# Product g by seven smaller products in ten chunks, w_out's sums by accumulating DMAs, and an instruction order worked out at build time

## The chip, the cores and the metric

One core of a Trainium2 chip runs the kernel. The metric is the time on the device in microseconds (us): the median of three runs of the kernel before is 777.73 us (777.39 to 778.22). PE is the matrix engine, DVE, ACT and POOL are the vector, scalar and GpSimd engines, and SP is the engine that issues nearly all DMAs.

## The reference

With DEPTH = 1 only the gated short convolution is computed, for 1024 tokens of width 1024, in float32:

```
u = x * rsqrt(mean(x*x) + eps) * pre_norm
z, bg, cg, v = split(u @ w_in, 4)              # w_in: 1024 x 8192, four parts of 2048 columns
y = bg * causal_conv3(cg * v) * silu(z)
m = y @ w_out                                  # w_out: 2048 x 1024
out = x + m * rsqrt(mean(m*m) + eps) * post_norm
```

## The kernel before

**Precision.** A float32 operand is split in a high part (a cast on ACT) and a low part (source minus high part, on DVE). One product of two operands is three matmuls: low by high, high by low, high by high. Where both inputs of the low part's subtraction would lie in SBUF, the kernel can first copy the source to a PSUM bank named `beside` on ACT (`split_by_bank`, lines 183 to 188), so that DVE reads one input from PSUM.

**Tiling of w_in.** The 2048 inner columns are 16 chunks c of 128. A chunk has two pairs p of weight blocks: p = 2c holds (cg, v), p = 2c+1 holds (z, bg). A pair is a 2 x 2 matrix (two column types by two halves of the 1024 rows), and so is u (two halves of the rows by two halves of the tokens). The 2 x 2 product is worked out with seven block products a to g instead of eight (`product`, line 215), on sums and differences of blocks. The sums of w (named se, sc, sf and the difference that overwrites a raw block) are made on POOL (`add_s`, lines 143 to 159). Each of the seven is 4 steps of k by 3 matmuls, 12 matmuls of 128 x 512, into a PSUM bank. What comes out is copied to SBUF by ACT (`snap`, 232) or added by DVE (`after`, from 241).

**One level deeper.** Products b (from chunk 2) and f (chunks 3 to 14) are themselves 2 x 2, over both pairs of a chunk, and are worked out by seven smaller products of 6 matmuls of 128 x 256 (`deep_product`, 779; sums of w on POOL in `deep_sums`, 746; splits in `deep_prep`, 761; results in `deep_after`, 802, and `deep_after_f`, 818). `by_seven` (172) says where. The deeper operands of u stand in tiles with the tag `ub`.

**After a chunk.** The gate cg times v is written in `gpad` (line 281), three convolution taps go over 1024 columns (one on ACT, 674, two on DVE, 683), and products with bg and silu(z) give y's chunk, which goes to DRAM (`y_done`, 290). w_out's product has the same form (seven block products, two of them one level deeper), so sums of y's chunks are made on DVE (`add_y`, 302) and stored.

**w_out's sums.** They do not depend on x. In pairs 8 to 23 `fetch_t` (320) loads rows of w_out, and `add_t` (332) makes the sums: for the large products d, e, g and c by 32 subtractions of 128 x 512 on DVE (355), each stored to DRAM (`t_d`), for the deeper ones by 256-wide subtractions on POOL (342 to 350). They are read again at the end (`load_unit`, 847).

**Order.** The scheduler is switched off: each engine's instructions stand in the order in which the Python code calls them. The order of PE's products is the list `slots` (line 958), and `prepare` (1003) calls the splits of w 7 us ahead of their slot. Buffers of 128 x 512 words come from one pool of PAGES = 36 pages; an instruction or a load that needs a page waits until one is free. After the last pair comes w_out's product (`out_mm`, 1130, and `small_mm`, 1213), with its loads, splits and the second norm in `BESIDE` (1297). SP issues all loads and stores from one queue, in order.

Of the kernel before, what the change touches and what calls it, by code (L numbers as in the profile page):

```python
# [1 line left out]

# [6 lines left out]
F32 = mybir.dt.float32  # L9
# [6 lines left out]
PAGES = 36  # L16
DEEP = 2
DEEP_F = 3
LEAD = 7.0
BY_BANK_DEEP = (("b", 0), ("b", 1), ("b", 2), ("f", 0), ("f", 2))  # L20


@with_exitstack
def kernel(
# [16 lines left out]
    nc = tc.nc  # L41
# [19 lines left out]
    const = ctx.enter_context(tc.tile_pool(name="const", bufs=1))  # L61
    small = ctx.enter_context(tc.tile_pool(name="small", bufs=2))
    up = ctx.enter_context(tc.tile_pool(name="up", bufs=7))
    pages = ctx.enter_context(tc.tile_pool(name="pages", bufs=PAGES))
    psum = ctx.enter_context(tc.tile_pool(name="psum", bufs=8, space=bass.MemoryType.PSUM))
    dram = ctx.enter_context(tc.tile_pool(name="dram", bufs=1, space=bass.MemoryType.DRAM))
# [27 lines left out]
    tx_d = dram.tile([P, 2, CQ, HB // 2], F32, tag="tx_d", name="tx_d")  # L94

# [75 lines left out]

    def by_seven(z, c):

        return c >= DEEP if z == "b" else DEEP_F <= c < NC - 1

# [65 lines left out]
    def after(p, i):  # L241
# [9 lines left out]
        elif i == "d":  # L251
            t = sn[p, "e"]
            nc.vector.tensor_add(t, x_, t)
            if p % 2 and DEEP <= c < DEEP_F:
                for j in range(1, TAPS):
                    conv_tap(c, j)
            elif p == len(PAIRS) - 1 or p % 2 and by_seven("f", c):
                conv_tap(c, TAPS - 1)
            if p % 2:
                nc.gpsimd.tensor_mul(t, t, cvs[c][:, HB:])  # L260
# [10 lines left out]
        elif i == "g":  # L271
            if p % 2:
                cv = cvs[c][:, :HB]
                nc.vector.tensor_mul(cv, x_, cv)
                nc.vector.tensor_mul(cv, cv, sn[p, "a"])
                y_done(c, cvs.pop(c))
            elif c < DEEP:
                start_conv(c)

# [22 lines left out]
    def add_y(c):  # L302
# [6 lines left out]
        else:  # L309
            cv, (t0, t1) = done.pop(c), far_y.pop(c)  # L310
            t2 = page(f"s4_{c}")
            nc.vector.tensor_add(t1, t1, cv[:, HB:])
            nc.vector.tensor_sub(t0, t1, t0)
            nc.vector.tensor_sub(t2, cv[:, :HB], t0)
# [5 lines left out]
    def fetch_t(j):  # L320

        if j >= CH:
            z, k = divmod(j - CH, CQ)
            ts[j] = [page(f"tb{n}_{j}") for n in (0, 1)]
            for n in (0, 1):
                nc.sync.dma_start(ts[j][n], wov[:, CH + k + n * CQ, z * HB : (z + 1) * HB])
            return
        ts[j] = [page(f"t{n}_{j}") for n in range(4)]
        for n, t in enumerate(ts[j]):
            nc.sync.dma_start(t, wov[:, j + n // 2 * CH, n % 2 * HB : (n % 2 + 1) * HB])  # L330

    def add_t(j, steps=range(4)):

        if j >= CH:
            z, k = divmod(j - CH, CQ)
            if 0 in steps:
                ts[j].append(page(f"t23_{j}"))
            b0, b1, t = ts[j]
            l, r = slice(0, HB // 2), slice(HB // 2, HB)
            for n in steps:  # L340
                if n == 0:
                    nc.gpsimd.tensor_sub(b0[:, r], b0[:, r], b0[:, l])
                    nc.sync.dma_start(tb_d[:, z, 0, k], b0)
                elif n == 1:
                    nc.gpsimd.tensor_sub(t[:, l], b1[:, r], b0[:, r])
                elif n == 2:
                    nc.gpsimd.tensor_sub(t[:, r], t[:, l], b0[:, l])
                    nc.sync.dma_start(tb_d[:, z, 1, k], t)
                else:
                    nc.gpsimd.tensor_sub(b1[:, l], b1[:, l], t[:, l])  # L350
                    nc.sync.dma_start(tx_d[:, z, k], b1[:, l])
            return
        t = ts[j]
# [999 lines left out]
```

## Time and profile before

| what | value |
|---|---|
| median of three runs | 777.73 us |
| span of the profiled execution, first to last instruction | 776.2 us |
| median less span | 1.5 us |
| busy: PE, DVE, ACT, POOL | 766.0, 618.4, 436.3, 413.2 us |
| matmuls recorded | 4086 |
| moved by DMA | 127.17 MB, mean 164 GB/s |
| granted PE clock over the span | 0.997 |

No time of the profiled execution itself is given apart from its span; the span and the 1.5 us around it stand for it. A row of the timeline reads: start in us from the span's first instruction, length in us, engine, line, operation, output <- inputs, number of merged instructions, and in brackets the idle time before it with what ended it. A row of the groups has, after the bar, busy us and mean ns of one. A row of the windows gives, for one stretch, its length and the busy us of PE, PE's weight loads, DVE, ACT and POOL, the granted clock, the DMA engines' share and GB/s.

### The profile page before, as it was taken

What the parts mean: (1) busy time and instruction counts of PE and PEld (TensorE: products, weight loads), DVE (VectorE), ACT (ScalarE), POOL (GpSimd) and SP (SyncE); (2) the same over time, 40 slices, a digit from 0 to 9 for tenths busy, and PEclk for the clock granted to TensorE, in tenths of its full rate; (3) what the DMA queues carried; (4) which work ended last, traced back from release to release, by engine and by line L of the source; (5) the groups of instructions that cost most, each with busy time, mean ns of one, the idle gap of its engine ahead of it and who ended that gap; (6) DMA issues with size and microseconds to landing.
All of it is one profiled execution on the core that took longest, in us unless ns stands there. A gap on an engine that the chain in (4) does not pass through costs nothing.

```text
span 776.2 us, 12058 instructions
## 1 busy us (share of the span) xinstructions
PE 766.0 (99%) x4086; PEld 661.8 (85%) x4086; DVE 618.4 (80%) x934; ACT 436.3 (56%) x810; POOL 413.2 (53%) x369
## 2 busy tenths in 40 slices
PE   8999999999999999999999999999999999999996
PEld 6888888888888888888888888888888889889985
DVE  5899786778687878788888887676778899966975
ACT  6764354766556565546465556555544576753821
POOL 2506786937575757575767667373737100850041
PEclk9999999999999999999999999999999999999998
DMA  9210531335463637364847456232325989966345
GB/s 310 71 55 1 149 96 55 96 109 181 138 204 117 210 111 230 111 208 131 257 136 250 138 174 178 96 109 96 115 89 166 336 275 378 309 196 210 112 169 184
DMA packets 115965, 127.17 MB, mean 164 GB/s; under 512 B 7432, under 2 KB 74304, under 8 KB 115904
## 3 DMA queue, kind: packets, MB, share of 16 engines
q1 hardware_dynamic: 115888, 126.41, 50.5%
q8 instruction: 32, 0.52, 0.3%
q14 instruction: 29, 0.24, 0.1%
q10 hardware_dynamic: 16, 0.00, 0.0%
HBM read 91.78 MB, written 34.60 MB: 163 GB/s over the span
## 4 chain that ended last, share of the span: by engine, by line
PE 98%; DVE 1%; DMA 1%; ACT 0%; POOL 0%; issue 0%; POOLq 0%; DVEq 0%; ACTq 0%
PE px L226 15%; PE px L227 15%; PE px L228 15%; PE pv L226 4%; PE pv L227 4%; PE pv L228 4%; PE po_x L1139 4%; PE po_x L1140 4%; PE po_x L1138 4%; PE px2b L800 2%; PE px2b L798 2%; PE px2b L799 2%; PE px2f L800 1%; PE px2f L799 1%; PE px2f L798 1%; PE pp L456 1%
## 5 line engine op out<-in xcount | busy, mean ns | idle before, releaser
L260 POOL TENSOR_TENSOR sne<-sne,cv 128x512 f32<-128x512 f32 x15 | 20.5, 1369 | 122.3 <-DVE cv L683 106.4
L187 ACT COPY beside<-raw 128x512 f32<-128x512 f32 x84 | 49.6, 590 | 29.2 <-DVE dwb1l L188 21.7
L154 POOL TENSOR_TENSOR se<-raw,raw 128x512 f32<-128x512 f32 x31 | 46.8, 1510 | 19.2 <-PE px L228 6.8
L234 ACT COPY sna<-px 128x512 f32<-128x512 f32 x30 | 17.6, 588 | 68.8 <-PE px L228 68.1
L226 PE MATMUL px<-u_d,wdl 128*128 128x512 f32 x124 | 48.7, 393 | 0.0
L226 PE MATMUL px<-u_a,wal 128*128 128x512 f32 x124 | 48.6, 392 | 0.0
L227 PE MATMUL px<-u_a,wah 128*128 128x512 f32 x124 | 48.6, 392 | 0.0
L227 PE MATMUL px<-u_d,wdh 128*128 128x512 f32 x124 | 48.5, 391 | 0.0
L226 PE MATMUL px<-u_g,wgl 128*128 128x512 f32 x124 | 48.4, 391 | 0.0
L227 PE MATMUL px<-u_g,wgh 128*128 128x512 f32 x124 | 48.4, 391 | 0.0
L227 PE MATMUL pv<-u_e,weh 128*128 128x512 f32 x124 | 48.4, 390 | 0.0
L228 PE MATMUL px<-u_d,wdh 128*128 128x512 f32 x124 | 48.4, 390 | 0.0
L226 PE MATMUL pv<-u_e,wel 128*128 128x512 f32 x124 | 48.4, 390 | 0.0
L228 PE MATMUL px<-u_a,wah 128*128 128x512 f32 x124 | 48.3, 389 | 0.0
L227 PE MATMUL px<-u_c,wch 128*128 128x512 f32 x124 | 48.2, 389 | 0.0
L228 PE MATMUL px<-u_c,wch 128*128 128x512 f32 x124 | 48.2, 389 | 0.0
L228 PE MATMUL pv<-u_e,weh 128*128 128x512 f32 x124 | 48.2, 389 | 0.0
L226 PE MATMUL px<-u_c,wcl 128*128 128x512 f32 x124 | 48.2, 389 | 0.0
L228 PE MATMUL px<-u_g,wgh 128*128 128x512 f32 x124 | 48.2, 389 | 0.0
L156 POOL TENSOR_TENSOR sc<-se,raw 128x512 f32<-128x512 f32 x31 | 44.9, 1448 | 5.8 <-issue 3.4
L158 POOL TENSOR_TENSOR sf<-raw,sc 128x512 f32<-128x512 f32 x31 | 46.3, 1493 | 0.0
L355 DVE TENSOR_TENSOR t<-t,t 128x512 f32<-128x512 f32 x32 | 45.8, 1450 | 0.3
(539 smaller groups left out, 2743.7 us busy)
## 6 DMA issues: line engine op xcount, KB each, us to landing
raw<-in_sc_w_in SPq DMA_DIRECT2D x128, 256.0 KB, 4.0
y_d<-cv SPq DMA_DIRECT2D x16, 512.0 KB, 3.2
s_d<-s SPq DMA_DIRECT2D x32, 256.0 KB, 2.9
t<-in_sc_w_out SPq DMA_DIRECT2D x32, 256.0 KB, 2.9
t_d<-t SPq DMA_DIRECT2D x32, 256.0 KB, 3.9
tb<-in_sc_w_out SPq DMA_DIRECT2D x16, 256.0 KB, 4.3
s<-y_d SPq DMA_DIRECT2D x16, 256.0 KB, 4.1
xr<-in_x SPq DMA_DIRECT2D x16, 256.0 KB, 3.8
```

What stands on the lines that cost most here:

```text
L154: nc.gpsimd.tensor_add(t, block(p, 1, 0), block(p, 1, 1))
L156: nc.gpsimd.tensor_sub(t, sums[p, "e"], block(p, 0, 0))
L158: nc.gpsimd.tensor_sub(t, block(p, 0, 1), sums[p, "c"])
L187: nc.scalar.copy(b, src)
L226: nc.tensor.matmul(ps, lo, UH[i][:, k], start=first and k == 0, stop=False, skip_group_check=True)
L227: nc.tensor.matmul(ps, hi, UL[i][:, k], start=False, stop=False, skip_group_check=True)
L228: nc.tensor.matmul(ps, hi, UH[i][:, k], start=False, stop=last, skip_group_check=True)
L355: nc.vector.tensor_sub(t[n], t[a], t[b])
L798: nc.tensor.matmul(ps, lo, uh, start=first and k == 0, stop=False, skip_group_check=True)
L1138: nc.tensor.matmul(ps, lo, u[:, 0, k], start=first, stop=False, skip_group_check=True)
L1139: nc.tensor.matmul(ps, hi, u[:, 1, k], start=False, stop=False, skip_group_check=True)
L1140: nc.tensor.matmul(ps, hi, u[:, 0, k], start=False, stop=last, skip_group_check=True)
```

## The change

**Product g deeper.** g is worked out by seven smaller products too, in chunks 4 to 13. Three of the seven (b', f', g') accumulate straight into the bank of the pair's x product, the other four are copied out and added back to that bank:

```diff
+LAST = {"b": NC, "f": NC - 1, "g": NC - 2}
 def by_seven(z, c):
-    return c >= DEEP if z == "b" else DEEP_F <= c < NC - 1
+    return {"b": DEEP, "f": DEEP_F, "g": DEEP_G}[z] <= c < LAST[z]
...
+elif z == "g" and i in ("b'", "f'", "g'"):
+    ps, first = banks[2 * c + (i == "g'"), "x"][:, HH if i == "f'" else 0 :], False
...
+def deep_after_g(c, i):
+    if i == "g'" and late_conv(c):
+        conv_tap(c, 1)
+    if i in ("b'", "f'", "g'"):
+        return
+    ps = banks[c, "g" + DEEP_C[i][0]][:, :HH]
+    if i == "d'":
+        t, x_ = page(f"gs1_{c}"), banks[2 * c + 1, "x"]
+        nc.scalar.copy(t[:, :HH], ps)
+        nc.vector.tensor_add(t[:, HH:], banks[c, "gv'"][:, :HH], t[:, :HH])
+        nc.vector.tensor_add(x_, x_, t)
+        ...
```

The sums of w for it are four more 256-wide subtractions or additions per chunk on POOL, its splits are plain ones (both inputs in SBUF). Its operands of u are six more `ub` buffers (14 to 20), and PAGES falls from 36 to 30. One of them overwrites a quarter of u_g, which is kept in DRAM (`ug_d`, stored once from SBUF) and restored after chunk 13. In chunks 4 to 13 the gate, the taps and the last products of a chunk come in the next chunk's first pair (`late_conv`).

**w_out's sums.** The 32 loads, 32 subtractions on DVE and 32 stores are gone. `sums_plan` spreads over pairs 9 to 25 (8 sums, each a half of one of e, d, c, g) one DRAM-to-DRAM copy on SP of 1 MB and two DMAs of 512 KB issued by POOL that add in DRAM:

```diff
+def out_sums(p):
+    for to, src, more in SUM_AT.get(p, ()):
+        if more:
+            nc.gpsimd.dma_start(to, src, accum_op=ALU.add)
+        else:
+            nc.sync.dma_start(to, src)
```

Sums take the place of differences, so signs turn: `add_y` uses scalar_tensor_tensor with -1.0 for two of its three steps, and one more ACT instruction multiplies half of the post norm's weights by -1.

**Order.** A class `Plan` stands in front of the engines. From the first planned slot (pair 2) to the end of the last pair it records the calls, works out a due time for each, and issues them in the order of a list scheduling with assumed durations, limited by free pages and PSUM banks; PE's order stays as recorded. Its assumptions, cut:

```diff
+LATE = {"end": 14.0, "store": 6.0, "psum": 3.0}
+SLACK = {"tensor": 1.0, "gpsimd": 0.8, "sync": 1.0, "scalar": 0.1, "vector": 0.1}
+AHEAD = {"sync": 24.0, "gpsimd": 18.0, "scalar": 11.0, "vector": 11.0}
+    ISSUE = {"sync": 0.07, "gpsimd": 1.2, "scalar": 0.1}
...
+    elif where == "tensor":
+        op.dur, op.lat = n / 2400 + 0.0135, n / 2400 + 0.2
+    elif where == "vector":
+        op.dur = 0.1 + n / 960 * (1 if psum or two else 0.55)
+        op.share = 0.0 if psum or not two else 0.4
+    elif where == "scalar":
+        op.dur = 0.1 + n / 1200
+    else:
+        op.dur = 0.16 + n / 390 if n > 8 else 0.1
...
+    if e == "gpsimd" and "dma" in op.name[1]:
+        self.sum_at = t + 15.0
```

The head (norm, transposes, first chunks) and w_out's product keep the order of the calls. Counted in the two built programs: 240 matmuls of 128 x 512 go and 420 of 128 x 256 come; DVE has 33 instructions more (32 subtractions for w_out and 20 low parts of g gone, 30 low parts of 128 x 512, 10 of 128 x 256, 20 sums of 128 x 256 and 20 of 128 x 512 come, and a few for u_g); ACT has 48 more; POOL has 52 compute instructions (four per chunk, four for one further set of sums that no product reads, eight for u_g) and 16 DMA issues more; SP has 50 DMA issues fewer.

More of the change, by code (lines that the diff above doesn't have):

```diff
@@ new lines, with __init__, tile @@
+class Pool:
+    def __init__(self, plan, pool, bufs, space):
+        self.plan, self.pool, self.bufs, self.space, self.gate, self.users = plan, pool, bufs, space, None, []
+    def tile(self, shape, dtype, **kw):
+        t = Tile(self, list(shape), dtype, kw)
+        self.plan.room.setdefault(t.key, kw.get("bufs", self.bufs))
+        if not self.plan.recording:
+            t.get()
+            self.plan.taken.setdefault(t.key, []).append(t)
+        return t
+class Op:
+    __slots__ = ("engine", "name", "args", "kw", "n", "needs", "feeds", "dur", "lat", "waits", "late", "tiles", "news", "start", "ideal", "pos", "share", "soft")
@@ L34 @@
 ):
-    nc = tc.nc
+    nc = plan = Plan(tc.nc)
     P = 128
```

574 lines of the change are left out of this document (471 added, 103 removed).

## The prediction

> **What bounds the kernel now.** I read the page first: the busy times, then the chain that ended last.
>
> ```profile
> span 776.2 us, 12058 instructions
> PE 766.0 (99%) x4086; PEld 661.8 (85%) x4086; DVE 618.4 (80%) x934; ACT 436.3 (56%) x810; POOL 413.2 (53%) x369
> PE 98%; DVE 1%; DMA 1%; ACT 0%; POOL 0%; issue 0%; POOLq 0%; DVEq 0%; ACTq 0%
> ```
>
> PE carries 98% of the chain. A busy PE alone does not prove a gapless PE, so the windows come next: a long one that leaves out head and tail, then two in the middle and one at the start of w_out's product.
>
> ```profile
> core 0: us, PE busy (x) PEld busy (x) DVE busy (x) ACT busy (x) POOL busy (x), PEclk, DMA share, GB/s
> 25.60:770.00 744.40, 744.22 (x3969) 643.71 (x3968) 598.83 (x893) 416.38 (x775) 407.79 (x355) 1.00 0.50 160
> 220.00:260.00 40.00, 40.00 (x220) 34.81 (x219) 32.50 (x47) 22.11 (x40) 27.38 (x26) 1.00 0.55 179
> 460.00:500.00 40.00, 40.00 (x224) 34.97 (x223) 28.93 (x45) 22.41 (x41) 25.89 (x25) 1.00 0.46 142
> 620.00:655.00 35.00, 35.00 (x206) 31.14 (x206) 33.14 (x61) 21.49 (x40) 1.29 (x1) 1.00 0.88 310
> ```
>
> In 744.40 us PE lacks 0.18 us, at a granted clock of 1.00. No wait is left to remove there. Two things follow. A gain can only come from fewer or cheaper matmuls, and what any other engine saves is worth nothing by itself. And every wait that the change brings to PE is added in full. The price of a matmul is its distance to the next one, not its recorded length (0.39 us, which overlaps), so I take starts from the timeline:
>
> ```profile
> 582.76 0.39 PE L226 MATMUL px<-u_g,wgl 128*128 128x512 f32 x1
> 585.48 0.39 PE L226 MATMUL px<-u_c,wcl 128*128 128x512 f32 x1
> 590.92 0.28 PE L798 MATMUL px2b<-u_b,dwb0l 128*128 128x256 f32 x1
> 592.36 0.40 PE L226 MATMUL px<-u_d,wdl 128*128 128x512 f32 x1
> 600.54 0.28 PE L798 MATMUL px2b<-ubch_deep,dwb1l 128*128 128x256 f32 x1
> 601.96 0.40 PE L226 MATMUL px<-u_g,wgl 128*128 128x512 f32 x1
> 610.15 0.28 PE L798 MATMUL pv2b<-u_b,dwb2l 128*128 128x256 f32 x1
> 611.57 0.40 PE L226 MATMUL px<-u_d,wdl 128*128 128x512 f32 x1
> ```
>
> Product g, 12 matmuls of 512, lasts from 582.76 to 585.48, 2.72 us. In the smaller form, a' and b' (12 matmuls of 256) take 1.44 us, c' and e' 1.42, f' and d' 1.42.
>
> **The change on PE.** Per chunk g goes twice: 2 x 2.72 = 5.44 us. Seven small products come, with the operands arranged as for b: 1.44 + 1.42 + 1.42 and half of 1.42 for g', 4.99 us. That is 0.45 us less, 4.5 us in ten chunks. Head, w_out's product and the finish after the last matmul keep their matmuls. If PE stays gapless the span is 776.2 - 4.5 = 771.7 us. The median of the runs lies 777.73 - 776.2 = 1.5 us above the span, so 773.2 us. If all seven cost 0.71 the saving is 4.7, if all cost 0.72 it is 4.0.
>
> All else counts only if PE must wait for it, so the question for each engine is whether its work per chunk still fits in a chunk. A chunk's period now is 37.33 us (POOL's se rows below, 215.36 to 252.69); it becomes 36.88.
>
> **POOL** gets most. Its rows, one chunk of them, and DVE's rows beside:
>
> ```profile
> 215.36 1.75 POOL L154 TENSOR_TENSOR se<-raw,raw 128x512 f32<-128x512 f32 x1
> 222.29 1.07 POOL L752 TENSOR_TENSOR dsf<-sf 128x256 f32<-128x256 f32 x1
> 230.68 1.30 POOL L154 TENSOR_TENSOR se<-raw,raw 128x512 f32<-128x512 f32 x1 [1.52 <-DVE dwb2l L188]
> 235.82 0.92 POOL L342 TENSOR_TENSOR tb<-tb 128x256 f32<-128x256 f32 x1
> 238.40 0.74 POOL L350 TENSOR_TENSOR tb<-tb,t 128x256 f32<-128x256 f32 x1
> 246.80 1.31 POOL L260 TENSOR_TENSOR sne<-sne,cv 128x512 f32<-128x512 f32 x1 [7.66 <-DVE cv L683]
> 248.47 1.35 POOL L1086 TENSOR_TENSOR cv<-snc,sne 128x512 f32<-128x512 f32 x1 [0.35 <-ACT snc L1085]
> 249.78 0.74 POOL L752 TENSOR_TENSOR dsb<-raw 128x256 f32<-128x256 f32 x1
> 252.69 1.74 POOL L154 TENSOR_TENSOR se<-raw,raw 128x512 f32<-128x512 f32 x1
> L355 DVE TENSOR_TENSOR t<-t,t 128x512 f32<-128x512 f32 x32 | 45.8, 1450 | 0.3
> 216.48 2.88 DVE L355 TENSOR_TENSOR t<-t,t 128x512 f32<-128x512 f32 x2
> 225.55 0.68 DVE L192 TENSOR_TENSOR wcl<-sc,wch 128x512 fp32r<-128x512 f32 x1
> 243.65 1.28 DVE L683 SCALAR_TENSOR_TENSOR cv<-gpad,cw,cv 128x1024 f32<-128x1024 f32 x1
> 235.71 0.43 DVE L163 TENSOR_TENSOR dwb<-raw,dwb 128x256 fp32r<-128x256 f32 x1
> L805 DVE TENSOR_TENSOR sna<-px2b,sna 128x256 f32<-128x256 f32 x56 | 23.3, 416 | 3.9 <-PE px2b L800 3.8
> L188 DVE TENSOR_TENSOR wgl<-beside,wgh 128x512 fp32r<-128x512 f32 x24 | 16.4, 685 | 3.9 <-ACT beside L187 3.9
> ```
>
> Four 512-wide sums take 5.14 us (230.68 to 235.82), but 6.93 (215.36 to 222.29) where DVE works on w_out's sums, which themselves take 1.45 us instead of the 0.68 of an equal subtraction (wcl). So an instruction of DVE with two inputs in SBUF and one of POOL hold each other up: 1.79 us on POOL for four of 0.68 us, two thirds of their time. Undisturbed, POOL's chunk is 2 x 5.14 for the sums, 8 x 0.73 for the deeper ones (four from 249.78 to 252.69), 3.3 for tb, and three products of at most 1.35: 23.4 us. By the window it was busy 27.38 x 37.33 / 40 = 25.6, so 2.2 us are disturbance. The g sums add 4 x 0.73 = 2.9. The disturbers change little: 4 x 0.68 = 2.7 us of w_out's sums go, three low parts of 0.68 and one of 0.43 come, 2.5 us. That makes 28.5 us of 36.88.
>
> On top come the 16 accumulating DMAs, two per chunk in chunks 5 to 12. The trace has no DMA that POOL issues. The bounds for its hold on POOL's queue: from below an issue on SP, 1.85 us for four, 0.46 each; from above the landing of a load, 6.0 us, if the queue stood until then (rows below). A negative price is out, since an instruction is added. I take 1.75, the slowest 512-wide POOL row: the instruction stands in POOL's queue like those, and between ends far apart theirs is the nearest row. That is 3.5 us, 32.0 of 36.88 us, and PE feels nothing. If the price is p, POOL is full at p = (36.88 - 28.5) / 2 = 4.2 us; beyond that each further us costs 2 us in each of eight chunks, 16 us.
>
> The Trainium skill, "SBUF — State Buffer", section "Who interferes with whom", says that a DVE instruction with two SBUF inputs and a GpSimd instruction that reads SBUF block each other completely; the two thirds of the rows lean that way.
>
> **DVE.** Out of a chunk go 4 x 1.45 and two low parts of 0.69, 7.2 us. In come 3 x 0.68 + 0.43, two sums of 0.42 (as L805) and two of 0.69 that add to the bank, 4.7; if a disturbed low part takes as long as POOL's slowest row, 1.75, it is 7.9. DVE's 32.50 x 37.33 / 40 = 30.3 us become 27.8 to 31.0 of 36.88. In chunks 12 and 13, which had no such sums, 28.93 x 37.33 / 40 = 27.0 becomes 30.3 to 33.5. It fits.
>
> **ACT** was at 22.11 of 40. Two casts and two copies per chunk go, four casts and three 256-wide copies come, about 1 us: free.
>
> **SP and DMA.** 50 issues fewer, and about the same bytes in the middle, at a DMA share of 0.55: free. A 1 MB copy holds the loads of w behind it back by a few us; the plan lets SP issue up to 24 us ahead of a due time (AHEAD), which covers a copy and a landing of 6.0 us (row B_b below).
>
> **Six pages fewer.** In w_out's product DVE frees a page with each low part, four in 2.48 us (row oy_a), 0.62 each, so a load may start 6 x 0.62 = 3.7 us later. The tightest load there:
>
> ```profile
> 591.25 1.85 SPq L858 DMA_DIRECT2D ru_a<-in_sc_w_out  x4
> B_b<-tb_d SPq DMA_DIRECT2D x8, 256.0 KB, 6.0
> 623.37 2.48 DVE L163 TENSOR_TENSOR oy_a<-ry_a,oy_a 128x512 fp32r<-128x512 f32 x4
> 626.94 1.81 SPq L917 DMA_DIRECT2D B_b<-tb_d  x4
> 642.50 2.18 ACT L162 CAST oB_b<-B_b 128x512 fp32r<-128x512 f32 x4 [4.24 <-DMA s_d<-s]
> ```
>
> Issued by 628.8 and landed 6.0 later, at 634.8, it is used at 642.5: 7.7 us cover 3.7. I cost the pages at nothing there; if that cover were gone, 3.7 us. In the middle the pages are a matter of order.
>
> **The order.** Before, POOL stood 7.66 us behind a tap (row 246.80); a recorded order by due times can fill that. Its assumed durations are near the rows: POOL 512-wide 0.16 + 512/390 = 1.47 against 1.30 to 1.75, DVE 0.63 against 0.68, a matmul 0.227 against 2.72/12 = 0.227. Its margins (0.8 to 1 us for what POOL, SP and PE hand over) are wider than these errors. I cost it at 0, between a gain that PE cannot show and one late operand per chunk.
>
> **The rivals.**
>
> *Part of it is given back.* PE waits 0.15 to 0.3 us per chunk for a low part or a free bank, since four results of g' now pass by ACT and DVE and back into the bank that the next products need, and since DVE runs up to 33.5 of 36.88 us. At 0.3 that is 3 us, 776.2. Against it: the other engines have an eighth or more of the period free.
>
> *All of it is given back*: 0.45 us per chunk, or the 3.7 us of the pages, gives 777 to 778. Also here: the copies and waits behind g' make PE wait exactly where b and f did not.
>
> *POOL becomes the bound.* If it is disturbed by every DVE instruction with two SBUF inputs, as in the four rows at 215.36, and not only by few, its chunk is 23.4 + 2.9 + 2/3 x 11.1 = 33.7 us. The 11.1 are DVE's instructions of that kind after the change: e's and c's low parts (4 x 0.68), two taps (2 x 1.28), three others of 0.68, three of 0.43, and 2.5 for g. Then p above 1.6 us decides. At p = 2.5 a chunk lacks 1.8 us, eight chunks 14 us: 773.2 + 14 = 787 us, slower. Whole blocking instead of two thirds adds 3.7 us to each chunk. For it: the disturbance is in the rows, and issuing is unmeasured. Against it: in the old chunk, with 11.3 us of the same kind and POOL 69% busy, only 2.2 us of disturbance came.
>
> The far end of this rival is that the two exclude each other wholly, wherever they meet. POOL and those DVE instructions then share one time: 26.3 + 11.1 = 37.4 us, over the period even without the DMAs. With p = 1.75 a chunk lacks 4.0 us, eight chunks 32 us, 805 us. The old chunk, 23.4 + 11.3 = 34.7 of 37.33, does not refute it. I give it 5 in 100, within the rival's 25. The rule of the Trainium skill cited above is this far end.
>
> **How the numbers follow.** Forecast, PE gapless within 1 us: 50 in 100, 773.2, its own range 772.4 to 774.3. Partly given back, 774.3 to 776.1: 14. All given back, 776.1 to 779.3: 11. POOL as the bound, above 779.3: 25. A measurement of this kernel can tell about 0.2%, 1.6 us, from no change, so below 776.1 is faster: 64; the same: 11; slower: 25. The range begins at 772.4 (below 773.2 by 0.5 of spread between runs and 0.2 for the cheaper small products, rounded out) and ends at 787, the rival's price at p = 2.5, which leaves out about 15.
>
> **What would show it.** Right: 420 matmuls of 256 with 0.118 to 0.120 us between starts, PE without gaps from 26 us on, its last matmul 4.5 us earlier; POOL at some 32 of 37 us in the middle. Wrong: gaps on PE that end with a low part of se, sc or g late behind a POOL sum (POOL the bound), or behind a load (pages), or with an addition to the x bank (given back). A POOL queue that stands several us at each accumulating DMA would upset the sum most.

## The result and the profile after

The changed kernel takes 791.86 us (median of five runs, 791.77 to 792.4) against 777.73 us for the kernel before on the same chip: 1.0183 times as long, 95% interval 1.0171 to 1.0196. It is slower by 14 us where 773.2 us was forecast, and it lies above the forecast range (772.4 to 787.0). The page of the changed kernel begins with these lines. In this kernel every instruction is issued through `Plan.call`, so all of them carry line 182, and the rows are told apart by their tiles.

```profile
span 790.4 us, 12619 instructions
PE 766.5 (97%) x4266; PEld 666.8 (84%) x4266; DVE 654.5 (83%) x967; ACT 450.0 (57%) x858; POOL 493.5 (62%) x437
```

The windows answer to those of before: the same stretch from 25.60 us to 6.2 us ahead of the span's end, two in the middle, and the start of w_out's product.

```profile
core 0: us, PE busy (x) PEld busy (x) DVE busy (x) ACT busy (x) POOL busy (x), PEclk, DMA share, GB/s
25.60:784.20 758.60, 743.72 (x4148) 647.89 (x4146) 634.38 (x925) 429.68 (x823) 487.81 (x423) 1.00 0.53 160
220.00:260.00 40.00, 37.78 (x227) 33.30 (x226) 35.23 (x51) 22.34 (x43) 32.56 (x30) 1.00 0.57 155
460.00:500.00 40.00, 38.13 (x227) 33.51 (x226) 34.21 (x51) 21.64 (x41) 34.35 (x31) 1.00 0.53 136
634.00:669.00 35.00, 35.00 (x206) 31.15 (x205) 33.12 (x60) 20.39 (x39) 1.47 (x1) 1.00 0.88 299
```

The stretch is 758.60 - 744.40 = 14.2 us longer at the same clock, and PE is no longer gapless in the middle: 2.2 and 1.9 us are missing in the two windows of 40 us. In w_out's product nothing is missing. So the gain is not absent; waits have been put on top of it. With the 4.5 us of the prediction's sum there must be 14.2 + 4.5 = 18.7 us of new waits. The view of waits, rows of PE's weight loads outside the head, has them (tile that waited, what it waited for, us in total, times, longest):

```profile
PEld pv2f L182 <- DVE snc L182: 11.1, 7, 1.8
PEld px2f L182 <- DVE dwf1l L182: 4.5, 5, 1.4
PEld px L182 <- DVE wcl L182: 1.9, 1, 1.9
PEld px L182 <- DVE wgl L182: 1.0, 1, 1.0
```

They add up to 18.5 us, and so do the distances between the starts of PE's matmuls, less what they show in the kernel before. (PE's recorded idle time is smaller, 14.9 us of the stretch, since the record of a matmul, 0.39 us, covers a part of the wait behind it.) In the kernel before none of these four rows exists. The largest is one wait seven times over, once in each of the chunks 5 to 11. Here is one of them in the timeline, first POOL and then DVE and PE:

```profile
232.10 1.74 POOL L182 TENSOR_TENSOR raw<-raw,raw 128x512 f32<-128x512 f32 x1
233.78 1.20 POOL L182 DMA_DIRECT2D t_d<-in_sc_w_out  x1
234.54 1.22 POOL L182 TENSOR_TENSOR dsg<-raw 128x256 f32<-128x256 f32 x1
235.24 1.21 POOL L182 TENSOR_TENSOR dsg<-raw,raw 128x256 f32<-128x256 f32 x1
235.94 1.20 POOL L182 TENSOR_TENSOR dsg<-dsg,raw 128x256 f32<-128x256 f32 x1
237.51 1.65 POOL L182 TENSOR_TENSOR se<-raw,raw 128x512 f32<-128x512 f32 x1 [0.37 <-DVE dwf L182]
234.05 3.38 DVE L182 TENSOR_TENSOR dwf<-sf,dwf 128x256 fp32r<-128x256 f32 x1
237.35 0.68 DVE L182 TENSOR_TENSOR dwg0l<-raw,dwg0h 128x512 fp32r<-128x512 f32 x1
237.95 0.41 DVE L182 TENSOR_TENSOR snc<-px2f,snc 128x256 f32<-128x256 f32 x1
238.29 0.67 DVE L182 TENSOR_TENSOR dwf2l<-beside,dwf2h 128x512 fp32r<-128x512 f32 x1
238.88 0.41 DVE L182 TENSOR_TENSOR snc<-pv2f,snc 128x256 f32<-128x256 f32 x1
239.35 0.38 PE L182 MATMUL pv2f<-u_f,dwf2l 128*128 128x256 f32 x1 [1.48 <-DVE snc L182]
```

The reader is to see five things. POOL issues an accumulating DMA at 233.78, and its three sums for product g follow without a gap, 0.70 us from start to start, though each is recorded with 1.2 us. DVE's low part `dwf` (both inputs in SBUF) starts at 234.05 and takes 3.38 us; it ends with the third sum. Behind it in DVE's queue stands, four places on, the addition that reads the bank pv2f. PE has to write that bank next and waits 1.48 us. And POOL itself then waits for `dwf`, which is what ends its series. The row of this tile over the whole kernel gives minimum, median and maximum of its twelve in ns:

```profile
L182 DVE TENSOR_TENSOR dwf<-sf,dwf x12: 412/3354/3380, 159.0 to 582.0; 128x256 fp32r<-128x256 f32 x12
```

Three take 0.41 to 0.43 us, two 0.96, and seven 3.35 to 3.38. The other places are smaller. At px2f a low part (dwf1l) comes late because the POOL sum it splits (dsf) is late. The early one looks like this:

```profile
59.67 0.10 POOL L182 MEMSET gpad<- 128x2 f32 x1 [23.99 <-DMA ug_d<-xa]
63.39 1.31 DVE L182 TENSOR_TENSOR wel<-se,weh 128x512 fp32r<-128x512 f32 x1 [0.40 <-ACT weh L182]
64.62 1.76 DVE L182 TENSOR_TENSOR wcl<-sc,wch 128x512 fp32r<-128x512 f32 x1
66.44 0.50 PE L182 MATMUL px<-u_c,wcl 128*128 128x512 f32 x1 [1.50 <-DVE wcl L182]
```

POOL's memset waits for the landing of the new store of u_g, and the worked-out order has wel ahead of wcl, which PE needs first. At 576 us the low part wgl stands behind three sums of y in DVE's queue.

### The profile page after: what moved, and what is told of

Read it like the earlier page. It is cut to its first block, busy times and chain, and to the rows that moved or that the text cites. A ratio compares the mean times of both kernels' runs of the same rounds, so it can differ in the third digit from the quotient of the medians.

```text
span 790.4 us, 12619 instructions
## 1 busy us (share of the span) xinstructions
PE 766.5 (97%) x4266; PEld 666.8 (84%) x4266; DVE 654.5 (83%) x967; ACT 450.0 (57%) x858; POOL 493.5 (62%) x437
## 5 line engine op out<-in xcount | busy, mean ns | idle before, releaser
L182 PE MATMUL px<-u_d,wdh 128*128 128x512 f32 x248 | 76.8, 391 | 0.0
L182 PE MATMUL px<-u_a,wah 128*128 128x512 f32 x248 | 76.7, 390 | 0.0
L182 PE MATMUL pv<-u_e,weh 128*128 128x512 f32 x248 | 76.6, 390 | 0.0
L182 PE MATMUL px<-u_c,wch 128*128 128x512 f32 x248 | 76.6, 390 | 0.0
L182 PEld LDWEIGHTS px<-u_d,wdh 128*128 128x128 f32 x248 | 46.6, 188 | 9.3 <-DVE u_d L182 0.2
L182 DVE SCALAR_TENSOR_TENSOR cv<-gpad,cw,cv 128x1024 f32<-128x1024 f32 x32 | 46.8, 1463 | 9.1 <-ACT cv L182 9.1
L182 PEld LDWEIGHTS px<-u_c,wch 128*128 128x128 f32 x248 | 46.7, 188 | 9.1
L182 PEld LDWEIGHTS pv<-u_e,weh 128*128 128x128 f32 x248 | 46.6, 188 | 9.1
L182 PEld LDWEIGHTS px<-u_a,wah 128*128 128x128 f32 x248 | 46.7, 188 | 8.9
L182 POOL TENSOR_TENSOR raw<-raw,raw 128x512 f32<-128x512 f32 x31 | 48.3, 1560 | 0.0
```

Of the source, the lines that this page charges most:

```text
L182: getattr(engine, name)(*(self.plain(a) for a in args), **{k: self.plain(a) for k, a in kw.items()})
```

## The experiments

**Theories.** *Held*: the accumulating DMA, followed at once by POOL sums, keeps a DVE instruction with two SBUF inputs out until the series ends, and DVE's order passes it to PE. Rivals: *Series* (the sums that follow each other do it without a DMA), *Load* (POOL has too much to do, the DMA is beside the point), and for the other 8 us *order* against *load*. Most runs keep the changed kernel's worked-out order and alter it only where `flush` issues it, so that nothing else moves; c1_bank, c2_head, c3_gap and the three runs with a d have their order worked out anew.

**Without POOL's DMAs (a1_no_dma).**

```diff
 for op in order:
+    if op.engine == "gpsimd" and "dma" in op.name[1]:
+        continue
```

> Same instructions in the same order as the changed kernel, except that POOL's 16 accumulating DMAs are left out (the sums of w_out's rows are incomplete, half of each addition is missing). Held (a DMA issued by POOL, followed at once by POOL sums, holds up a DVE instruction with two SBUF inputs until the series ends, and PE gets that through the pv2f bank): dwf falls from 3.38 us to at most 1.5 us, the seven stalls at pv2f (10.8 us) go, 779 to 782 us. Series (the sums that follow each other do it without a DMA): dwf stays above 2.5 us, 790 to 792 us. Load (POOL has too much to do, whatever it is): some 0.8 us of POOL per DMA goes, the stalls behind POOL's late sums shrink all over, those at px2f (3.2 us) as much as those at pv2f: below 779 us.

Measured: 779.54 us (778.84 to 780.02), 12.3 us less, in a kernel that leaves out half of each addition of w_out's rows. The groups of this run (us in all and mean ns before and after the comma) have this row for `dwf`:

```profile
L182 DVE TENSOR_TENSOR dwf<-sf,dwf 128x256 fp32r<-128x256 f32 x12 | 9.9, 823 | 0.0
```

and its waits of PE's weight loads between 200 and 600 us these:

```profile
PEld px2f L182 <- DVE dwf1l L182: 2.2, 3, 0.7
PEld px L182 <- DVE wgl L182: 1.0, 1, 1.0
```

`dwf` falls from 26.7 us in all to 9.9, and the row of pv2f is gone. The sums of g still follow each other without a gap on POOL: Series is refuted. The waits at px2f fall only from 4.5 to 2.2 us, so the DMA's own time on POOL is a small part.

**POOL work in the DMA's place (a2_stand_in).**

```diff
+    if op.engine == "gpsimd" and "dma" in op.name[1]:
+        op.name[0].tensor_sub(*self.scratch)
+        op.name[0].tensor_sub(*self.scratch)
+        continue
```

> In place of each of POOL's 16 DMAs stand two POOL subtractions of 128x224 in SBUF, some 0.65 us each, so POOL has at least as much to do at the same places; w_out's sums are incomplete. Held: no DMA, no hold, dwf at most 1.5 us, no stall at pv2f of over 0.5 us, 779 to 783 us. Series: more sums in a row hold DVE longer, dwf 3.4 us or more, 791 to 794 us. Load: POOL as full as before, 790 to 793 us, whatever dwf takes.

Measured: 784.62 us (784.29 to 785.23). No wait at pv2f and no DVE instruction longer than 1.3 us above its usual time: Load doesn't make the seven waits. But it is 5.1 us more than without the stand-ins, a little outside what Held expected: the waits at px2f rise from 2.2 to 7.1 us in the row of the weight loads. POOL's queue is tight ahead of dsf, where 1.3 us more of anything reach PE.

**Copying instead of adding (a3_plain_dma).**

```diff
+    if op.engine == "gpsimd" and "dma" in op.name[1]:
+        op.kw = {}
```

> POOL's 16 DMAs stay in place with the same rows but copy instead of adding (w_out's sums hold one addend only). Held, by the issue on POOL: dwf stays at 3.4 us, 790 to 792 us. If it is the addition (longer landing, DRAM read and written) that counts: dwf at most 1.5 us and 779 to 782 us. Series and Load: 790 to 792 us, which this run does not tell from Held.

Measured: 787.68 us (787.35 to 788.11). `dwf` takes 2.91 us in the seven chunks, the waits at pv2f are 7.6 us. The time lies between the two forecasts: the hold is there, a little shorter, and the DMA is recorded with 0.73 us instead of 1.19. So in this kernel it is not the adding alone that holds.

**The DMA eight places later (a4_dma_later).** In the order, POOL's DMA ahead of the dsg sums is moved behind the next pair's difference, ahead of sf:

```diff
+    j = next(n for n in pool if any(s.startswith("sf_") for s in names(order[n])))
+    order.insert(j - 1, order.pop(k))
```

> Same instructions, nothing left out; the DMA that POOL issues ahead of the dsg sums (eight of the 16) stands instead behind the next pair's difference, ahead of sf, where POOL has some 4.7 us of idle time. Held: dwf at most 1.5 us, the seven stalls at pv2f go, 779 to 783 us. Series: dwf stays above 2.5 us, 790 to 792 us. Load: POOL's work per chunk is the same, only eight DMAs stand later; the sums ahead come 0.8 us sooner, so part of the stalls goes, 785 to 790 us.

Measured: 788.82 us (788.06 to 789.53), far from the 779 to 783 that Held had. The seven waits at pv2f are gone, but now the second DMA of each chunk waits for the first, POOL has no idle time left behind it, and the hold is there again at another place:

```profile
289.28 1.15 POOL L182 DMA_DIRECT2D t_d<-in_sc_w_out  x1 [4.77 <-issue]
295.90 1.11 POOL L182 TENSOR_TENSOR t<-tb,tb 128x256 f32<-128x256 f32 x1
294.03 4.07 DVE L182 SCALAR_TENSOR_TENSOR cv<-gpad,cw,cv 128x1024 f32<-128x1024 f32 x1 [0.40 <-ACT cv L182]
```

Between the first two rows POOL made six sums without a gap, and a tap of the convolution, 1.28 us when alone, waited for the last of them. In four chunks a tap took 4.0 to 4.8 us. So Held has to be put more widely: not the instruction beside the DMA is held, but any in the series that the DMA begins.

**The disputed instruction by itself (b1_measure, b2_sweep, b3_before).** A program of its own: POOL and DVE start on the same ACT instruction, POOL issues nothing, a copying or an accumulating DMA and then makes subtractions, and DVE makes a 128x256 addition.

```diff
+nc.gpsimd.dma_start(dst[:, case], wov[...], accum_op=ALU.add)
+for n in range(count):
+    nc.gpsimd.tensor_sub(outs[n], a[:, :256], a[:, 256:])
+for _ in range(delay):
+    nc.vector.tensor_add(pp, ps[:, :256], b[:, 256:])   # reads PSUM, 0.46 us apart
+nc.vector.tensor_sub(v, b[:, :256], b[:, 256:])
```

> A program of its own that measures the disputed instruction alone and computes nothing of the reference (the output is a copy of x). In each case DVE starts a 128x256 addition of two SBUF tiles while POOL issues no DMA, a copying DMA or an accumulating DMA of 512 KB in DRAM, and then makes 1, 2, 3, 4, 6 or 8 subtractions of 128x256 in a row (some 0.7 us each); a second set gives DVE one PSUM input. Held: without a DMA the addition takes at most about 1.3 us, however many subtractions; with a DMA it takes about 0.7 us per subtraction more, 2.0 at one, 3.4 at three, 6.9 at eight; with a PSUM input 0.41 us always. Series: it grows with the count without a DMA as well. If neither: at most 1.3 us in all cases, and the 3.4 us of the changed kernel have another cause.

It missed the case: with either DMA DVE's addition started ahead of it and was over before the sums (0.41 to 0.42 us; 0.90 to 0.97 without a DMA). The sweep moves it:

> A program of its own, like the first measurement (nothing of the reference is computed, the output is a copy of x), but DVE's addition of two SBUF tiles, 128x256, starts later by 0.34 us per step, so that it falls into POOL's DMA or among the 8 subtractions behind it; in the first measurement it ended before them. Held in the series: an addition that starts among or ahead of the subtractions behind a DMA takes until the last of them, up to 6 us; without a DMA at most 1.1 us (what is left of one subtraction, and 0.41). With 2 and 4 subtractions it ends with those. If a memset between the DMA and the subtractions ends the hold, at most 1.1 us there, else as without it. A PSUM input: 0.41. The rule that the one that issues first has the pair for its own instruction alone: at most 1.1 us in every case.

The timeline of the sweep, POOL's DMA and series for the first held case, then DVE (the name says kind and number of subtractions; pp are the additions that read PSUM and delay the start):

```profile
160.75 1.15 POOL L56 DMA_DIRECT2D dst<-in_sc_w_out  x1 [0.37 <-issue]
161.52 5.85 POOL L60 TENSOR_TENSOR o<-a 128x256 f32<-128x256 f32 x8
51.34 0.95 DVE L64 TENSOR_TENSOR none8late<-b 128x256 f32<-128x256 f32 x1
105.53 0.91 DVE L64 TENSOR_TENSOR plain8late<-b 128x256 f32<-128x256 f32 x1
161.87 5.79 DVE L64 TENSOR_TENSOR accum8late<-b 128x256 f32<-128x256 f32 x1
204.25 3.62 DVE L63 TENSOR_TENSOR pp<-ps,b 128x256 f32<-128x256 f32 x8
207.79 3.97 DVE L64 TENSOR_TENSOR accum8late<-b 128x256 f32<-128x256 f32 x1
230.87 1.77 DVE L64 TENSOR_TENSOR accum2late<-b 128x256 f32<-128x256 f32 x1
253.10 3.12 DVE L64 TENSOR_TENSOR accum4late<-b 128x256 f32<-128x256 f32 x1
```

An addition that starts among the subtractions behind an accumulating DMA ends 0.3 us after the last of them (161.87 + 5.79 = 167.66 against 161.52 + 5.85 = 167.37), however many there are; in the two starts between it takes 5.4 and 4.9 us. Without a DMA it waits for what is left of one subtraction. With a PSUM input it isn't held: the eight additions from 204.25 on run on at 0.46 us each, though POOL's series begins at 205.59, and the one with two SBUF inputs behind them is caught. A memset between DMA and subtractions doesn't help (5.2 us). The Trainium skill, "SBUF — State Buffer", section "Who interferes with whom", calls the pair of ports that DVE and POOL share an exclusive lock and gives it to whichever issues first, for its whole instruction (it says the latter of DVE's two-port modes). The rows without a DMA agree, at most 0.97 us; the rows behind an accumulating DMA don't, since there DVE waits for up to eight instructions of POOL. Why it waits no run shows.

One thing differs from the kernel. In the two sweeps an addition that started during the accumulating DMA, ahead of the first subtraction, was not held (0.44 to 0.93 us). In the kernel `dwf` starts 0.27 us behind the DMA and 0.49 us ahead of the first sum, and is held. So the programs show that such a series holds DVE, but not every condition for it.

Two questions were left, the copying DMA and what ends a hold:

> A program of its own again (the output is a copy of x): as the sweep, but two subtractions stand ahead of the DMA without a pause, as the difference does in the changed kernel, and six behind it; four cases have a POOL copy that waits for ACT behind three subtractions, and five more subtractions behind that. If the issue on POOL is enough, whatever it does, the copying DMA holds the addition to the end of the series here as the accumulating one does (2.9 us in the changed kernel with copying DMAs), which it did not when POOL was idle ahead of it. If only the accumulating DMA holds, the copying one leaves at most 1.1 us. A pause that POOL makes ends a hold: an addition that starts among the first three takes until the pause, 2 us at most, and one that starts behind the pause at most 1.1 us.

```profile
95.73 0.91 DVE L70 TENSOR_TENSOR plain6late<-b 128x256 f32<-128x256 f32 x1
177.81 4.45 DVE L70 TENSOR_TENSOR accum6late<-b 128x256 f32<-128x256 f32 x1
234.90 2.44 DVE L70 TENSOR_TENSOR pause3late<-b 128x256 f32<-128x256 f32 x1
272.15 0.84 DVE L70 TENSOR_TENSOR pause3late<-b 128x256 f32<-128x256 f32 x1
```

A copying DMA holds nothing here (0.46 to 0.95 us in seven starts). A pause of POOL (here 1.3 us or more) ends the hold: 2.44 us up to it, 0.84 behind it. Why the copying DMA held `dwf` for 2.91 us in the kernel stays open.

**The low part by way of PSUM (c1_bank).**

```diff
-BY_BANK_DEEP = (("b", 0), ("b", 1), ("b", 2), ("f", 0), ("f", 2))
+BY_BANK_DEEP = (("b", 0), ("b", 1), ("b", 2), ("f", 0), ("f", 2), ("f", 3))
```

> Nothing left out. The low part of f's g' operand (dwf, 128x256) is read by way of the PSUM bank, so that DVE needs no second SBUF input there; the order is worked out anew with that. Held: dwf takes 0.41 us, the seven stalls at pv2f shrink to under 0.5 us each, the rest stays (3 us at px2f, 2.4 us early, 1.0 us late): 781 to 785 us; should the next DVE instruction with two SBUF inputs (dwg0l, right behind) be caught instead, 789 to 792 us. Load: POOL's work is unchanged, 790 to 792 us.

Measured: 814.26 us (813.3 to 815.85). `dwf` is free, and the next two-input instruction is caught, and for longer: `dwg0l` takes 5.5 us in three chunks and 7.2 in three more. POOL's `se` waits for `dwf` and so ended the old series; nothing in the series waits for `dwg0l`, so in these last three chunks it runs on over eight instructions.

**Earlier sums ahead of the memset (c2_head).**

```diff
+    add_s(2, "ec")
     head.close()
...
-            add_s(2, "ecdf")
+            add_s(2, "df")
```

> Nothing left out. se and sc of pair 2 are made ahead of the memset of gpad, which waits for the store of u_g; the order behind it is worked out anew. Early stall by that wait: the 2.35 us between 40 and 80 us fall below 0.7 us, the rest stays: 789.5 to 790.5 us. If the stall comes from DVE's order alone (wel ahead of wcl): 791 to 792.5 us.

Measured: 791.9 us (791.1 to 792.02). The early wait is split: by the starts of PE's matmuls 1.8 us between 40 and 80 us instead of 2.3, now at 57.3 and 59.6 us, where PE waits for DVE's low parts of u_g while POOL makes these sums. The memset alone is not the cause.

**DMAs only where POOL will pause (c3_gap).** `pick` may issue a DMA only if no other POOL instruction is due and ready within 1.3 us, and the sums begin at pair 3:

```diff
+if e == "gpsimd" and "dma" in op.name[1] and not pause(op):
+    continue
...
-sums_plan(2 * DEEP_F + 4)
+sums_plan(4)
```

> Nothing left out. POOL's 16 DMAs are all there, but the order is worked out with one more rule: POOL issues one only where none of its other instructions is due and ready within the next 1.3 us, and they may begin at pair 3 instead of 9, so that each chunk has one at a place where POOL then waits. Held in the series: no DVE instruction with two SBUF inputs over 1.5 us, no stall at pv2f, 778 to 781 us. Load: POOL has the same work in all, one DMA less per chunk: 784 to 789 us. A hold by any DMA, wherever it stands: 790 to 792 us.

Measured: 790.29 us (787.42 to 791.86), in the range of "a hold by any DMA". But no DVE instruction is held (none over 1.3 us above its usual time), and yet the time is about that of the changed kernel: in the new order POOL runs without a pause from 329 to 353 us, its dsf is late, and the waits at px2f are 7.6 us. It tells nothing against the hold, but it shows that an order without holds can lose as much elsewhere.

**DMAs sooner (d1_soon).**

```diff
-self.sum_at = t + 15.0
+self.sum_at = t + 9.0
...
-SUM_AT.setdefault(p0 + 2 * j + k, []).append(...)
+SUM_AT.setdefault(p0 + j, []).append(...)          # p0 = 3
```

> Nothing left out. POOL's 16 accumulating DMAs and their eight copies come sooner, two per pair in pairs 3 to 10 and at least 9 us apart, so that most of them lie in chunks 1 to 4, where POOL has less to do, and chunks 6 to 14 have none; the order is worked out anew. Held: a hold can still come in chunks 1 to 5, none later; the stalls at pv2f from 270 us on go, what stays is about that of the run without DMAs: 779 to 784 us. If POOL's time in the early chunks is as short as later: 784 to 790 us. Load with no part played by the DMAs: 790 to 792 us.

Measured: 809.52 us (808.67 to 809.69). Nine DVE instructions take 2.1 to 5.3 us, all behind DMAs in chunks 1 to 6; behind 280 us, where there are no DMAs, 3 us of waits are left. Held had forecast a gain of some 10 us, and a loss of 18 came: it failed in sign as well as in size. What fits it is only where the holds are. In the early chunks POOL's series were no shorter, so that more instructions than before were caught, nine instead of seven.

**g undone, and pages (d2_no_g, d3_no_g_36).**

```diff
-DEEP_G = 4
+DEEP_G = 99
...
-PAGES = 30
+PAGES = 36          # second run only, with 14 instead of 20 ub buffers
```

Both runs also leave out g's deeper operands of u and the store and restoring of u_g.

> Product g is worked out by twelve matmuls of 512 again in every chunk (its sums, splits, operands of u and the store of u_g are gone); POOL's DMAs, the worked-out order and 30 pages stay. Without waits it would take the 777.7 us of the kernel before. Held: dwf, dwg and dsg no longer meet behind a DMA as before, but other sums follow the DMAs; where a DVE instruction with two SBUF inputs meets them there are holds: 778 to 784 us, with holds seen in the trace if above 780. Order or pages alone make PE wait: 782 to 790 us without holds in the trace. If g's extra work is the cause of all stalls: 777 to 778.5 us.

> As the run with g undone, but with 36 pages instead of 30, which its smaller operands leave room for; the order is worked out anew. If POOL's waits for pages (sf behind the release of a page) make its sums late and PE wait, it is 1 us or more faster than with 30 pages; if pages cost nothing, within 1 us of it.

Measured: 782.79 us (780.8 to 784.22) with 30 pages, 779.88 us (779.66 to 779.98) with 36. The first is the case "order or pages alone", without holds in the trace. Both have all 16 DMAs and the worked-out order, and no hold: without the dsg sums pauses or other, mostly shorter series follow the DMAs. With 36 pages PE waits only early (1.3 us between 40 and 80 us), with 30 another 4 us at px2b between 280 and 400 us. So six pages fewer can cost some 3 us in the middle in this setting; whether they do so with g, no run shows.

**A pause, the order, and both (f1_pause, f2_rest, f3_all).** A POOL copy behind each such DMA that waits for `dwf`; three moves in the recorded order; both:

```diff
+self.call(op.name[0], "gpsimd", "tensor_copy", (self.hold, dwf_low[:, :1]), {})
...
+later("gpsimd", f"dsb1_{c}", f"dsf0_{c}")           # and ACT's casts of them
+later("vector", "wel_2", "wcl_2")                   # and ACT's casts
+later("vector", "s1_13", "wgl_28")
```

> The changed kernel's order, nothing left out and nothing moved; eight POOL instructions are added: behind each DMA that the dsg sums follow, POOL copies one element per partition of dwf's low part, so that it must wait until DVE has made dwf and its series is broken there. Held in the series: dwf ends during the DMA or right behind it (at most 1 us), the seven stalls at pv2f go, 780.5 to 783 us, with the stalls at px2f, early and at the end as they are. If the hold begins with the DMA itself and a pause doesn't end it, or if POOL's load is what counts: 791 us or more, since POOL has eight more waits.

> The changed kernel's order with three moves, nothing left out, the DMAs and the sums behind them untouched: f's first deeper sums (dsf0) and the cast of them ahead of b's second ones (dsb1); wcl ahead of wel in pair 2; wgl of chunk 14 ahead of y's sums. If the order among equals is what makes these operands late, the stalls at px2f (3.2 us), the early one (1.7 us of 2.4) and the one at 576 us (1.0 us) go: 786 to 787.5 us, and the seven stalls at pv2f stay. If POOL and DVE are simply too full there, the waits move elsewhere: 790 to 792 us.

> Both of these together: POOL's eight pauses and the three moves, nothing left out. If the causes are the ones named and add up, 791.9 less 10 less 5: 775.5 to 778 us, at or below the 777.7 us of the kernel before, and the matmuls' gain of 4.5 us comes out in part. If they don't add up (a wait that goes uncovers the next): 779 to 783 us.

Measured: 806.52 us (805.44 to 807.38), 812.21 us (808.26 to 814.85) and 803.17 us (802.19 to 804.27), 20 to 28 us above what the named causes gave. (The number of f1_pause lies in its range "791 us or more", but, as shown below, no pause came about there.) The timeline of f2_rest shows why:

```profile
397.81 1.17 POOL L182 DMA_DIRECT2D t_d<-in_sc_w_out  x1
398.56 1.19 POOL L182 TENSOR_TENSOR dsg<-raw 128x256 f32<-128x256 f32 x1
404.50 1.65 POOL L182 TENSOR_TENSOR raw<-raw,raw 128x512 f32<-128x512 f32 x1
399.33 7.38 DVE L182 TENSOR_TENSOR dwg0l<-raw,dwg0h 128x512 fp32r<-128x512 f32 x1
```

With operands sooner, `dwf` slips through ahead of the DMA and `dwg0l` is caught, as with the bank. In f1_pause `dwf` was already done when POOL came to its copy, so there was no pause (the sums follow 0.14 us later), and `dwg0l` took 7.2 us in three chunks, another low part (dwg1l) 3.7 us in two. The early wait (0.7 us left), those at px2f and the one at 576 us did go in f2_rest, as the order theory said.

A second loss comes on top in these three runs, in c1_bank and in d1_soon: behind PE's long waits the granted clock is lower. These are two windows of f2_rest, with the columns of the windows above, behind its wait of 5.1 us, which ends at 407.4 us (granted clock 0.61 and 0.70):

```profile
405.00:410.00 5.00, 2.64 (x6) 2.15 (x7) 4.33 (x7) 2.66 (x6) 1.15 (x1) 0.61 0.01 3
410.00:415.00 5.00, 5.00 (x26) 4.33 (x25) 4.68 (x10) 1.44 (x3) 0.47 (x1) 0.70 0.61 175
```

Matmuls of 512 columns then start 0.43 us apart instead of 0.23. In the five runs it happened behind 20 of the 21 waits of more than 2.8 us and cost some 5 to 12 us a run by the starts of the matmuls; the granted clock of the whole execution is 0.976 to 0.988. In the changed kernel the longest wait is 1.7 us, and no window of 5 us after the first 25 us shows a granted clock below 0.99. So the times of these five runs are not a measure of the holds alone.

**The moves without DMAs (g1_no_dma_order).** The three moves and the lines of a1_no_dma together.

> The run without POOL's 16 DMAs (w_out's sums incomplete, as there) and with the three moves of order on top (dsf0 ahead of dsb1, wcl ahead of wel, wgl ahead of y's sums). Without DMAs no hold; if the order of equals made the remaining stalls (early 2.4 us, at px2f 1.7 us, at 560 us 1.0 us, of which the moves took all in the run with the DMAs), 779.5 less 4 to 4.5: 774.5 to 776 us. If POOL and DVE are too full and the waits move: 778 to 780 us. Some hold without any DMA: above 780 us, with DVE rows over 2 us in the trace.

Measured: 775.12 us (774.87 to 775.16), 0.9966 of the kernel before (0.9953 to 0.9978), again without half of w_out's additions. Taken away in this sequence, the loss divides into 791.86 to 779.54 for the DMAs and 779.54 to 775.12 for the order. With the DMAs in place the same moves made the kernel slower (f2_rest), so the two don't simply add.

**DMAs at pauses, with the moves (g2_placed).** Three DMAs in the head, 13 behind sf of an even pair, where POOL pauses in the trace of g1_no_dma_order; SP's copies go out there too:

```diff
+plan.sums_at = {f"sf_{p}": sum_at(j) for j, p in enumerate([2, 6, 8, *range(12, 32, 2)], 3)}
```

> Everything is computed. The order of the run before (the changed kernel's order and the three moves), but POOL's 16 accumulating DMAs and SP's eight copies stand elsewhere: three in the head, behind sf of pair 1, where POOL then idles 24 us, and 13 behind sf of an even pair, where the trace of the run without DMAs shows POOL idle for 2.4 to 6 us before its next instruction (pair 10, with 1.3 us, is left out). Held in the series, and ended by a real pause: no DVE row over 1.5 us, DMAs cost nothing, 775 to 776.5 us, faster than the kernel before by 0.2 to 0.35%. If the sixteen DMAs cost by themselves (POOL's time, traffic beside the loads): 777 to 782 us. If a hold starts wherever a DMA stands: above 785 us.

Measured: 783.12 us (782.78 to 786.08), everything computed: 8.7 us faster than the changed kernel, 0.7% slower than the one before. It misses all three forecasts, by 1 us at the nearest (777 to 782, if the DMAs cost by themselves). No DVE instruction is over 1.2 us above its usual time, so the hold is gone with all DMAs in place. A part of what is left comes from a mistake in my placing, which SP's and POOL's rows of one chunk show:

```profile
433.20 0.48 SPq L182 DMA_DIRECT2D t_d<-t_d  x1
437.21 0.37 SPq L182 DMA_DIRECT2D raw<-in_sc_w_in  x1
445.92 0.74 POOL L182 TENSOR_TENSOR dsb<-raw 128x256 f32<-128x256 f32 x1 [3.70 <-DMA raw<-in_sc_w_in]
```

The 1 MB copy stands ahead of the chunk's last load of w, which lands 8.7 us after its issue. POOL stands idle for that load in all four chunks with a copy of this kind (4.9, 4.3, 3.7 and 2.4 us at 292, 369, 446 and 521 us); in the chunks between, with an accumulating DMA but no copy, it doesn't wait for it at 250 and 328 us, 0.3 us at 405, but 2.1 us at 483. In the changed kernel the copies went out behind the loads. Of 9.6 us of waits of PE behind 200 us, 5.9 come within 16 us of the four late loads; the other 3.7 have causes that no run separates. A placing with that mended was not run, so no version shown here computes everything and beats the kernel before.

## Why the prediction was wrong

*PE is gapless, so every wait counts in full.* Right: 18.5 us of waits, less 4.5, are the 14 us.

*The gain on PE.* Right. The starts of g's small products in the changed kernel:

```profile
245.74 0.28 PE L182 MATMUL px<-u_g,dwg0l 128*128 128x256 f32 x1
246.46 0.28 PE L182 MATMUL px2g<-u_g,dwg0l 128*128 128x256 f32 x1
250.64 0.28 PE L182 MATMUL px2g<-ugch_deep,dwg1l 128*128 128x256 f32 x1
251.35 0.28 PE L182 MATMUL pv2g<-u_g,dwg1l 128*128 128x256 f32 x1
```

0.72 and 0.71 us each, as taken. And g1_no_dma_order, with all of g's products though without half of w_out's additions, comes within 1.9 us of the 773.2.

*POOL's time.* Right in its sum and beside the point. 32.0 us per chunk were forecast; the window of 220 to 260 us has 32.56 of 40, 31.9 of a chunk that now takes 39.16 us (se at 213.44 to se at 252.60). The accumulating DMA takes 1.20 us and lets the next instruction start after 0.76, below the 1.75 that I took. **The step that failed is this one: "the instruction stands in POOL's queue like those", with "PE feels nothing" behind it.** I priced the DMA by the time it takes on its own engine, between 0.46 and 6.0 us, and asked only whether POOL is full at that price. Its price lay on another engine: DVE held for as long as POOL's series runs on, seven times 3 us, 11.1 us at PE. Where pauses or mostly shorter series followed it, PE showed no wait for it (d3_no_g_36). That the DMA and the series behind it do this is shown by runs; why they do is not.

*POOL becomes the bound* was the rival for the slower side. Its ingredients were right (POOL's DMA, DVE with two SBUF inputs, exclusion), its mechanism was not: POOL still idles 5.6 to 7.4 us in the windows of 40, and with stand-ins of at least equal length the seven waits don't come. The 25 in 100 for a slower kernel were right in sign only. No total of busy time, not even the far end of whole exclusion, describes a wait that depends on what stands behind what.

*DVE fits.* As a share it does: 35.23 of 40, some 3 of them held. Without holds (a1_no_dma) it was busy 348.2 of the 400 us from 200 to 600, 32.1 of 36.88, against the 27.8 to 31.0 of the sum. A low part was taken at 1.75 us at most, and seven took 3.35 to 3.38. But DVE works in order, and the addition that frees the bank pv2f stands four places behind `dwf`. The prediction named such a chain for g's additions, at 0.15 to 0.3 us a chunk, and not for f's, where it was 1.6 us.

*The order costs 0.* Wrong by 4.4 us (a1_no_dma against g1_no_dma_order): wel ahead of wcl, dsb1 ahead of dsf0, wgl behind y's sums. I compared the assumed durations with rows and didn't read the order itself against PE's.

*ACT, SP and six pages fewer are free.* In w_out's product, yes: the window of 634 to 669 us is full. In the middle it is open: six pages made 2.9 us with g undone. A copy of 1 MB does hold the load behind it, to a landing of 8.7 us in g2_placed, as the prediction said ("a few us").

*What would show it wrong* named gaps behind a late POOL sum, a load, or an addition to the x bank. The largest was none of these, but an addition that frees a bank, late through DVE's queue.

## What to carry over

The price of an instruction that the trace has never shown is not bounded by how long it may stand on its own engine; ask what it may do to other engines, and what stands in their queues behind the instruction it catches. With accumulating DMAs, leave POOL a real pause behind each. To let one DVE instruction read PSUM frees that one, but the next with two SBUF inputs is caught in its place (c1_bank). And with an order from a planner, read the order at the places where PE has no slack before costing it at nothing.

## What the runs showed of the hardware

A DVE instruction with two SBUF inputs that starts among POOL's instructions behind an accumulating DMA waits for the whole gapless series (1.8 us for two subtractions, 3.1 for four, 5.8 for eight in the sweep), against 0.97 us at most without a DMA there. A pause of 1.3 us or more ends it, a memset doesn't. In such a series POOL's 256-wide sums are recorded with 1.1 to 1.2 us at a distance of 0.70, so that the records overlap; in a3_plain_dma `dwf` was held with sums recorded at 0.75, so the overlap is no sure mark of a hold. An accumulating DMA of 512 KB takes 1.2 us on POOL, a copying one 0.73. Two accumulating ones don't overlap here: in the head of g2_placed, where POOL had nothing else to do, they were issued at 36.17, 42.78 and 49.55 us, each 0.3 us after the one before had landed. And behind 20 of 21 waits of PE of more than 2.8 us, in five runs, its matmuls of 512 columns started 0.43 us apart for a while instead of 0.23.
